# Seven block products for half of the output projection of an encoder block, with the last two gate groups regrouped

## Chip, cores and metric

The kernel runs on one core of a Trainium2 chip. The metric is device time of one execution in microseconds (us). A core has five engines that each run their own instructions in order and wait for one another by semaphores: PE (TensorE, matrix products), DVE (VectorE), ACT (ScalarE), POOL (GpSimd) and SP (SyncE, which here issues the transfers). PE writes into PSUM, eight banks of 512 f32 columns; the other engines must empty a bank before PE can write it again.

## The reference

One layer of an encoder block on 1024 tokens with 1024 channels, in f32:

```python
u = rms_norm(x, norm1_g)
proj = u @ w_in
q, k, v, cb, cc, ch, ga, gb = jnp.split(proj, split_pts, axis=-1)
...
y_a = neighbourhood_attention(q, k, v, rpb) @ w_attn_branch
y_b = short_gated_conv(cb, cc, ch, conv_w) @ w_conv_branch
merged = jax.nn.sigmoid(ga) * y_a + jax.nn.sigmoid(gb) * y_b
x = x + merged @ w_o
h = rms_norm(x, norm2_g) @ w_mlp_in
x = x + jnp.square(jax.nn.relu(h)) @ w_mlp_out
```

The change touches `merged` (gates and branches) and the product `merged @ w_o`, called the projection here: 1024 x 1024 by 1024 x 1024.

## The kernel before, in words

**Precision.** Every f32 operand is scaled by a power of two and split in two f16 parts, high and low. A product of two operands is three passes (high by high, high by low, low by high; `PASSES`, L479) that are added up in PSUM. The high part is an ACT copy with a scale, the low part a DVE `scalar_tensor_tensor` (scaled operand minus high part). A scale needs the largest element, or the sum of squares, of the whole operand over all 128 partitions: each engine makes a column of partial results, DVE casts it into a column of the tile `ones`, PE multiplies it by a matrix of ones (`all_sum`, L226, the matmul is L227), and DVE reads the sum back from PSUM (L230) and makes the power of two in four or five steps on single columns (`pow2`, L153, `pow2_half`, L467).

**Stages.** Input products, attention and short convolution; then eight gate groups n = 0..7 of 128 channels each; then the projection; then the two matrices of the MLP. Gate groups 1 to 7 and the MLP already use Strassen's scheme with seven products in place of eight (`seven`, L1273; one product is 12 matmuls of 512 or 256 columns); the projection doesn't.

**Gates.** For each n (L1342): seven products of 12 matmuls give both gates of the group for both halves of the tokens (`gate_units`, L1297). Their combination is on DVE (L1310 to L1313, L1319, L1326, L1327), the sigmoid on ACT (L1321). Then four branch groups of 12 matmuls (`branch_units`, L1331) give y_a and y_b of the group; DVE multiplies them by the gates (L1357) and adds the two (L1359) to `m`, the group's part of `merged`. `m_done` (L1290) takes the largest element of `m` and splits `m` into M[0] and M[1], the stationary operand of the projection, with a scale for each group. For n = 7 the four branch groups come first (L1368), the largest element is bounded from them (`bound`, L1373), and gate 7 comes last, so that its products can be multiplied in and split half by half (`last`, L1386).

**Weights.** Weights come as f32 pieces of 128 x 1024 into five rotating buffers `raw`; SP issues a load when an earlier piece has been split (`load_upto`, L261). w_o has two column halves of four pieces, cO[0] and cO[1]; each piece is reduced to its row maxima by DVE (`largest`, L357) and then split (L343, L330).

**Projection.** `proj(b, half)` (L1605): for a block b of 128 tokens and a half of 512 columns, 24 matmuls of 512 columns (8 channel groups, three passes), then DVE adds the result to x in X1 (L1610). The first half runs over b = 4, 5, 0, 1, 2, 6 (L1628 to L1635); channel group 7 of the first two blocks is put behind the other 42 matmuls. The ten other half-blocks (`tail`, L1637) run between the steps of the second norm, of `form_sums` (L1480), of the splits and transposes of the normalized rows, and of the first pieces of w_1 (`forms_m`, L1551; `prep1`, L1518).

**Order of the work.** Nothing is reordered after the program is written: each engine runs its instructions in the order in which the Python program emits them. Preparations are generators in two lists, `fg` and `bg`. `unit` (L233) emits one group of matmuls, then what was put off after the group before it (`late`: usually what empties its PSUM bank), and then moves `fg` by `steps` and `bg` by `ticks` steps. `apart` (L208) lets a generator wait for a count of groups before it emits its matmul with ones. `drain` and `flush` empty the lists. SP runs its transfers in the order of issue too, and one that waits holds those behind it.

Of the kernel before, what the change touches and what calls it, by code (L numbers as in the profile page):

```python
# [28 lines left out]
def plan():  # L29
# [9 lines left out]
    for n in range(8):  # L39
        p.append((("S" if n else "G", n), block("w_in", [(3072 + 128 * n, 128), (4096 + 128 * n, 128)], 4)))  # L40
        if n % 2 == 0:
            p += branch(n // 2)
# [57 lines left out]
def encoder_block(ctx: ExitStack, tc: tile.TileContext, x, weights, cols, gqk, rel, masks, out):  # L100
# [1183 lines left out]

    def m_split(n, m, s):
# [4 lines left out]
    def m_done(n, m):  # L1290
        mx, s = tmp(), tmp()
        V.tensor_reduce(sc[:, mx], m, axis=AX, op=OP.max, apply_absolute_value=True)
        yield
        yield from pow2(mx, 14, s, at(rowsM, n))
        yield from m_split(n, m, s)

    def gate_units(n, tail=None):  # L1297

        sg = w3p.tile([128, 4, 512], F32, name="sg")
# [18 lines left out]
        def post3(ps):  # L1318
# [9 lines left out]
            7: post7, 3: post3}, 2, 4 if n < 7 else 6, (1, 6, 2, 4, 5, 7, 3))  # L1328
        return sg

    def branch_units(n, post, mid=None):  # L1331
        j, cc = n // 2, (n % 2) * 128
        for g, act, ch in ((0, actA, cA[j]), (1, actB, cB[j])):
            built(ch)
            for half in range(2):
                ps = anybank()
                unit(ch_mms(ps, act, half, ch, 4, 256, cc),
                     lambda ps=ps, g=g, half=half, ch=ch: post(g, half, ps, sc[:, ch.inv]), 2, 4)
                if mid and g == 0 and half == 0:
                    mid()  # L1340

    for n in range(8):  # L1342
        built(cG if n == 0 else cS[n])
        if n < 7:
            bg.append(prep_s(n + 1))
        m = w3p.tile([128, 2, 512], F32, name="m", bufs=1)
        mf = m.rearrange("p a t -> p (a t)")
        if n < 7:
            sg = gate_units(n)
            if n:  # L1350
                sg = [sg[:, i] for i in range(4)]
            if n in (1, 3, 5):
                push(cA[n // 2 + 1], cB[n // 2 + 1])

            def post(g, half, ps, iv, sg=sg, m=m):
                t = sg[2 * half + g]
                V.scalar_tensor_tensor(t, ps, iv, t, op0=OP.mult, op1=OP.mult)  # L1357
                if g == 1:
                    V.tensor_tensor(m[:, half], sg[2 * half], t, op=OP.add)  # L1359
            branch_units(n, post, (lambda: turn_s(0, 2)) if n == 0 else None)  # L1360
            if n == 0:
                late.append(lambda: held.__setitem__(0, 0))
            late.append(lambda n=n, mf=mf: fg.append(m_done(n, mf)))
        else:
            push(cO[0])
            tick(4)
            y = w3p.tile([128, 4, 512], F32, name="gsum", bufs=1)
            branch_units(n, lambda g, half, ps, iv: A.activation(y[:, 2 * half + g], ps, AF.Copy, scale=iv))  # L1368
            settle()
            drain()  # L1370
            s7 = tmp()

            def bound():  # L1373
                mm, m2, mx = tmp(4), tmp(2), tmp()
                V.tensor_reduce(sc[:, mm], y, axis=AX, op=OP.max, apply_absolute_value=True)
                yield
                V.tensor_tensor(sc[:, m2], sc[:, mm.start:mm.start + 4:2], sc[:, mm.start + 1:mm.start + 4:2],
                                op=OP.add)
                V.tensor_reduce(sc[:, mx], sc[:, m2], axis=AX, op=OP.max)
                yield from pow2(mx, 14, s7, at(rowsM, 7))  # L1380
                for ch in cO:
                    ch.ready = True

            fg.append(bound())

            def last(sg, half):  # L1386
                o = slice(2 * half, 2 * half + 2)
                V.tensor_tensor(sg[:, o], sg[:, o], y[:, o], op=OP.mult)
                V.tensor_tensor(m[:, half], sg[:, 2 * half], sg[:, 2 * half + 1], op=OP.add)
                t = slice(512 * half, 512 * half + 512)  # L1390
                A.activation(M[0][:, 7, t], m[:, half], AF.Copy, scale=sc[:, s7])
                V.scalar_tensor_tensor(M[1][:, 7, t], m[:, half], sc[:, s7], M[0][:, 7, t],
                                       op0=OP.mult, op1=OP.subtract)

            gate_units(7, last)
            u2T = base.tile([128, 4, 2, 4, 512], F16, name="u2T", tag="U")
            c1[0].raw = [u2T[:, 3, i].rearrange("p k t -> p (k t)").bitcast(F32) for i in range(2)]
            for i in range(2):
                load_into(c1[0].raw[i], c1[0], i)
            r21 = u2T[:, 2, 0].rearrange("p k t -> p (k t)").bitcast(F32)  # L1400
            X1 = base.tile([128, 8, D], F32, name="x1", tag="Q")
            for b in range(8):
                SP.dma_start(X1[:, b], x[b * 128:(b + 1) * 128, :])
            load_into(r21, c1[1], 1)
            settle()
    drain()
    flush()
    side[0] = False

# [70 lines left out]
    def form_sums():  # L1480
        for _ in sums(fv[0], V):
            pass
# [543 lines left out]
```

## Time and profile before

| | |
|---|---|
| time, median of 3 runs | 1200.93 us (1200.65 to 1201.29) |
| the profiled execution's own time | 1201.78 us |
| its span, first to last instruction | 1200.0 us |
| granted PE clock | 1.00 throughout |

The profile is of one execution. Instructions carry the kernel's line (L1310), the engine, the operation, the tiles as out<-in, and the shape. In a timeline the columns are start and length in us; "x12" is the number of instructions merged in a row, and a bracket gives the engine's idle time before it with what ended it. In groups of instructions the last columns are busy us, mean ns of one, and idle time before. A matmul's end is modelled and reaches into the next one, so the distance between starts is the measure. Before, gate 7's first matmul starts at 514.33 and the projection's first at 532.48.

### The profile page before, as it was taken

What the parts mean: (1) busy time and instruction counts of PE and PEld (TensorE: products, weight loads), DVE (VectorE), ACT (ScalarE), POOL (GpSimd) and SP (SyncE); (2) the same over time, 40 slices, a digit from 0 to 9 for tenths busy, and PEclk for the clock granted to TensorE, in tenths of its full rate; (3) what the DMA queues carried; (4) which work ended last, traced back from release to release, by engine and by line L of the source; (5) the groups of instructions that cost most, each with busy time, mean ns of one, the idle gap of its engine ahead of it and who ended that gap; (6) DMA issues with size and microseconds to landing.
All of it is one profiled execution on the core that took longest, in us unless ns stands there. A gap on an engine that the chain in (4) does not pass through costs nothing.

```text
span 1200.0 us, 16982 instructions
## 1 busy us (share of the span) xinstructions
PE 1190.2 (99%) x6272; PEld 574.7 (48%) x6272; DVE 940.3 (78%) x1750; ACT 752.1 (63%) x1181; POOL 450.9 (38%) x296
## 2 busy tenths in 40 slices
PE   8999999999999999999999999999999999999998
PEld 7444444444444444444467444444444444444444
DVE  7987878899558786877888645645548999999998
ACT  7765668778654545337778778678675843746440
POOL 5610022322311203001014665565567561564562
DMA  7745547576641121234397445435466925435202
GB/s 259 201 153 126 107 96 145 124 163 117 135 121 58 54 70 36 71 116 165 60 170 195 174 142 192 160 130 193 153 242 220 356 73 193 158 120 214 105 36 105
DMA packets 162707, 171.25 MB, mean 143 GB/s; under 512 B 123328, under 2 KB 123840, under 8 KB 158528
## 3 DMA queue, kind: packets, MB, share of 16 engines
q1 hardware_dynamic: 162624, 170.17, 48.4%
q8 instruction: 49, 0.80, 0.3%
q14 instruction: 34, 0.28, 0.1%
HBM read 102.51 MB, written 37.75 MB: 117 GB/s over the span
## 4 chain that ended last, share of the span: by engine, by line
PE 84%; DVE 11%; ACT 2%; issue 1%; DMA 1%; SPq 0%; ACTq 0%
PE ps_d L236 27%; PE ps_s L236 24%; PE ps_o L236 20%; PE ps_d L1067 5%; PE ps_d L669 2%; PE ps_d L718 2%; PE ps_s L718 2%; DVE P L95 2%; PE ps_s L669 2%; DVE w_s L1234 1%; DVE sz L95 1%; DVE sc L95 1%; DVE w_ws L95 1%; DVE sg L1357 1%; DMA xt<-in_x 1%
## 5 line engine op out<-in xcount | busy, mean ns | idle before, releaser
L236 PEld LDWEIGHTS <-ops 128*128 128x128 f16 x1356 | 132.5, 98 | 157.3
L236 PEld LDWEIGHTS <-w 128*128 128x128 f16 x1368 | 132.8, 98 | 139.4
L1067 PE MATMUL ps_d<-uT,w_ws 128*128 128x512 f16 x576 | 128.0, 379 | 0.3 <-DVE cv L95 0.3
L236 PE MATMUL ps_s<-ops 128*128 128x512 f16 (+1 forms) x504 | 114.3, 376 | 0.0
L236 PE MATMUL ps_d<-ops 128*128 128x512 f16 x492 | 112.9, 379 | 0.0
L236 PE MATMUL ps_d<-u2T,w 128*128 128x512 f16 (+1 forms) x504 | 110.1, 371 | 0.0
L1847 ACT ACTIVATE ops<-hf,sc 128x2048 f16<-128x2048 f32 x26 | 52.0, 1998 | 84.8 <-PE ps_d L236 47.2
L1221 POOL TENSOR_TENSOR tsum<-raw 128x512 f32<-128x512 f32 x28 | 48.2, 1737 | 139.3 <-DVE v L1475 74.2
L1425 POOL TENSOR_TENSOR as<-as 128x512 f32<-128x512 f32 x60 | 82.9, 1382 | 41.6 <-ACT as L1707 38.1
L236 PEld LDWEIGHTS <-w_s 128*128 128x128 f16 x588 | 56.8, 98 | 69.0 <-DVE w_s L1234 1.2
L1067 PEld LDWEIGHTS <-w_ws 128*128 128x128 f16 x576 | 54.6, 98 | 65.6 <-issue 1.5
L236 PE MATMUL ps_o<-ops 128*128 128x512 f16 (+1 forms) x360 | 81.3, 375 | 0.0
L236 PE MATMUL ps_s<-u2x,w 128*128 128x512 f16 (+1 forms) x348 | 78.6, 375 | 0.0
L1849 DVE SCALAR_TENSOR_TENSOR ops<-hf,sc,ops 128x2048 f16<-128x2048 f32 x26 | 74.8, 2876 | 3.2 <-ACT ops L1847 2.2
L1099 ACT ACTIVATE raw<-raw,sc 128x256 f32<-128x256 f32 x164 | 67.5, 494 | 1.9 <-DMA raw<-in_weights 1.9
L1221 POOL TENSOR_TENSOR gsum<-raw 128x512 f32<-128x512 f32 x14 | 19.3, 1394 | 127.8 <-issue 53.6
L1238 ACT ACTIVATE w<-raw,sc 128x512 f16<-128x512 f32 (+1 forms) x28 | 24.6, 927 | 50.8 <-DVE sc L475 50.8
L1740 DVE TENSOR_TENSOR as<-ps_s,as 128x512 f32<-128x512 f32 x13 | 9.0, 692 | 57.9 <-ACT as L1759 57.9
L1321 ACT ACTIVATE sg<-sg,sc 128x2048 f32<-128x2048 f32 (+1 forms) x7 | 13.2, 1880 | 52.2 <-DVE sg L1319 52.2
L1863 POOL TENSOR_TENSOR raw<-raw 128x1024 f32<-128x1024 f32 x8 | 30.8, 3870 | 36.5 <-DVE ops L1857 36.5
L236 PE MATMUL ps_o<-u2T,w 128*128 128x512 f16 (+1 forms) x204 | 44.2, 366 | 0.0
L236 PEld LDWEIGHTS <-mH 128*128 128x128 f16 x304 | 29.6, 98 | 30.4
(393 smaller groups left out, 2664.2 us busy)
## 6 DMA issues: line engine op xcount, KB each, us to landing
raw<-in_weights SPq DMA_DIRECT2D x89, 512.0 KB, 5.2
hs<-as SPq DMA_DIRECT2D x16, 1792.0 KB, 8.7
hf<-hs SPq DMA_DIRECT2D x26, 1024.0 KB, 6.6
w2x<-in_weights SPq DMA_DIRECT2D x16, 512.0 KB, 7.6
raw<-in_weights SPq DMA_DIRECT2D x16, 384.0 KB, 3.7
xt<-in_x SPq DMA_DIRECT2D x8, 512.0 KB, 10.2
gs<-s SPq DMA_DIRECT2D x4, 1024.0 KB, 4.4
x<-in_x SPq DMA_DIRECT2D x8, 512.0 KB, 10.6
```

What stands on the lines that cost most here:

```text
L95: return f(out, *a, **kw)
L236: T.matmul(ps, l, r, start=a, stop=b)
L669: T.matmul(ps, UT[:, sa, k, b * 128:(b + 1) * 128], w, start=(kind, k) == ("hh", 0), stop=(kind, k) == ("hl", 7))
L718: T.matmul(vbank["q", b], UT[:, sa, k, b * 128:(b + 1) * 128], cQ.parts[:, sw, 512 * k:512 * k + 512], start=(k, n) == (0, 0), stop=(k, n) ...
L1067: T.matmul(ps, l, r, start=a, stop=b)
L1099: A.activation(v, v, AF.Copy, scale=sc[:, at(g, 4 * i + k)])
L1221: G.tensor_tensor(t[:, o], a, b, op=OP.add)
L1238: A.activation(o(0), w, AF.Copy, scale=sc[:, s])
L1425: sub.tensor_tensor(z[o], z[a], z[b], op=op)
L1847: A.activation(P[:, 1, 0], hf, AF.Copy, scale=sc[:, Rs])
L1849: V.scalar_tensor_tensor(P[:, 1, 1], hf, sc[:, Rs], P[:, 1, 0], op0=OP.mult, op1=OP.subtract)
L1863: G.tensor_tensor(w11[i2], w11[i2], w12[i2], op=OP.add)
```

## The change

1. **Branches of groups 6 and 7 first.** The loop over gate groups ends at n = 5. Then come all eight branch groups of n = 6 and 7 (`last_branches`), whose results are kept in four tiles `Y`, then gate 6 and gate 7 with no branches between them. Both are multiplied in half by half by `last`. The weights cA[3] and cB[3] are loaded ahead of gate 6's weights. `bound` now covers both groups.
2. **One scale for a pair of groups**, and Strassen's sums of `merged`: after each pair (2i, 2i+1) POOL forms four sums of 384 tokens in place (`m_sums`: they serve three of the four row blocks of each token half), ACT and DVE split them (`m_parts`), and SP stores them to memory in `MS`. Pairs 0, 1 and 2 are loaded again later; the sums of the last pair are made in `last_forms`, after gate 7, straight into their place. The gate tile `sg` has one buffer where it had two, and `m` holds a pair.
3. **w_o.** Scales come from sums of squares (ACT, `o_scale`), with the groups' scales applied afterwards, where they came from row maxima (DVE). The first half is split plain (`o_plain`, into the tile that held the convolution result) and, after four sums per piece on POOL, once more as sums (`W`). The second half (`prep_o1`) is prepared during the projection.
4. **Projection, first column half.** For the row pairs (0, 4), (1, 5), (2, 6): seven products in the order 1, 4, 2, 6, 7, 5, 3, each in two units of two row pairs and one, 12 matmuls of 256 columns for a row pair. `o_post` combines them into X1 on DVE, POOL and ACT. Row blocks 3 and 7 and the second column half stay as they were.
5. **Smaller moves.** The loads of w_1's first pieces (c1) go behind the third stored sum; w_1's first split waits for the end of the Strassen half (`o_half`) and takes another buffer; `form_sums` for three of four row pairs and the sums in `forms_m` go from DVE to POOL.

The core of the diff:

```diff
+    FORMS = ((3, 1, 3, OP.subtract), (1, 0, 1, OP.subtract), (0, 3, 0, OP.subtract), (2, 2, 0, OP.add))
...
+    def m_sums(m):
+        q = m.rearrange("p a h t -> p (a h) t")[:, :, 0:384]
+        for o, a, b, op in FORMS:
+            G.tensor_tensor(q[:, o], q[:, a], q[:, b], op=op)
+            yield
+        return q
+    def m_parts(q, t, s):
+        for a in (0, 2):
+            A.activation(t[:, a:a + 2, 0], q[:, a:a + 2], AF.Copy, scale=sc[:, s])
+            yield
+        for a in (0, 2):
+            V.scalar_tensor_tensor(t[:, a:a + 2, 1], q[:, a:a + 2], sc[:, s], t[:, a:a + 2, 0],
+                                   op0=OP.mult, op1=OP.subtract)
+            yield
...
+    def o_scale(ch, top, junk):
+        rm, rs, a, b, s = (cols_of("prep", i) for i in (4, 4, 1, 1, 1))
+        ch.inv = keep()
+        for p in range(4):
+            while len(ch.raw) <= p:
+                yield WAIT
+            A.activation(junk, ch.raw[p], AF.Square, accum_out=sc[:, at(rm, p)])
+            yield
+        while not o_ready[0]:
+            yield WAIT
+        ri = sc[:, rowsM.start:rowsM.start + 8:2]
+        for _ in range(2):
+            V.tensor_tensor(sc[:, rm], sc[:, rm], ri, op=OP.mult)
+        V.tensor_reduce(sc[:, a], sc[:, rm], axis=AX, op=OP.add)
+        c, mark = ones_col(), units[0]
+        V.tensor_copy(c, sc[:, a])
+        yield from apart(mark, 1)
+        yield from all_sum(c, b, anybank(), 1e-36)
+        yield from pow2_half(b, top, s, ch.inv)
+        V.tensor_scalar(sc[:, rs], ri, sc[:, s], None, op0=OP.mult)
+        yield
+        return rs
...
+    def prep_o():
...
+        for n in range(4):
+            yield from o_plain(ch, n, rs)
+            r = ch.raw[n].rearrange("p (f c) -> p f c", f=4)
+            for o, x_, y_ in ((0, 0, 1), (1, 1, 3), (3, 0, 3), (2, 3, 2)):
+                G.tensor_tensor(r[:, o], r[:, x_], r[:, y_], op=OP.add)
+            yield
+        while not gated[0]:
+            yield WAIT
+        W = wsp.tile([128, 4, 2, 1024], F16, name="w16_t", tag="ws")
+        WT.append(W)
+        for p in range(4):
+            r = ch.raw[p].rearrange("p (f c) -> p f c", f=4)
+            hi, lo = (W[:, :, w, 256 * p:256 * p + 256] for w in range(2))
+            A.activation(hi, r, AF.Copy, scale=sc[:, at(rs, p)])
+            yield
+            V.scalar_tensor_tensor(lo, r, sc[:, at(rs, p)], hi, op0=OP.mult, op1=OP.subtract)
+            done[0] += 1
+            load_upto(done[0] + 5)
+            yield
...
+    def last(n, m, sg, half):
+        V.tensor_tensor(sg[:, 2 * half], sg[:, 2 * half], Y[n, 0][:, half], op=OP.mult)
+        (G if n == 6 else V).tensor_tensor(sg[:, 2 * half + 1], sg[:, 2 * half + 1], Y[n, 1][:, half], op=OP.mult)
+        V.tensor_tensor(m[:, half], sg[:, 2 * half], sg[:, 2 * half + 1], op=OP.add)
+        if n == 7:
+            t = slice(512 * half, 512 * half + 512)
+            A.activation(M[0][:, 7, t], m[:, half], AF.Copy, scale=sc[:, s7])
+            V.scalar_tensor_tensor(M[1][:, 7, t], m[:, half], sc[:, s7], M[0][:, 7, t],
+                                   op0=OP.mult, op1=OP.subtract)
...
+    last_branches()
+    bg.append(prep_o())
+    settle()
+    fg.append(bound())
+    mp = w3p.tile([128, 2, 2, 512], F32, name="m", bufs=1)
+    built(cS[6])
+    gate_units(6, lambda sg, half: last(6, mp[:, 0], sg, half))
+    gated[0] = 1
+    built(cS[7])
+    late.append(lambda: fg.append(m_split(6, mp[:, 0].rearrange("p h t -> p (h t)"), s7)))
+    gate_units(7, lambda sg, half: last(7, mp[:, 1], sg, half))
...
+    for i in range(2):
+        SP.dma_start(SM[i], MS[:, i])
+    X1 = base.tile([128, 8, D], F32, name="x1", tag="Q")
+    for b in range(8):
+        SP.dma_start(X1[:, b], x[b * 128:(b + 1) * 128, :])
+    settle()
+    def last_forms():
+        q = yield from m_sums(mp)
+        yield from m_parts(q, SM[3], s7)
+        forming[0] += 1
+    fg.append(last_forms())
     drain()
...
+    SP.dma_start(SM[2], MS[:, 2])
+    for i in range(2):
+        load_into(c1[0].raw[i], c1[0], i)
+    load_into(r21, c1[1], 1)
...
-    push(cO[1])
+    bg.append(prep_o1())
...
+    PRODUCT = {1: (0, 0), 2: (1, 2), 4: (3, 6), 6: (4, 7), 7: (5, 5), 5: (7, 4), 3: (6, 3)}
...
+    for o in (1, 4, 2, 6, 7, 5, 3):
+        if o == 6:
+            while forming[0] < 4:
+                step()
+        for j, n in ((0, 2), (2, 1)):
+            ps = anybank()
+            mms = []
+            for c in range(n):
+                mms += o_mms(ps[:, 256 * c:256 * c + 256], o, j + c)
+            unit(mms, lambda ps=ps, o=o, j=j, n=n: o_post(o, ps, j, n, [acc[:, u, j:j + n] for u in range(3)]),
+                 5, 3 * n)
```

`PRODUCT` gives for each product its row sum and its weight sum. Row sums 0 to 3 are the plain parts of `merged` (even and odd channel group, first and second token half), 4 to 7 the sums of `m_sums`; weights 0 to 3 are plain quarters of a piece, 4 to 7 the sums in `W`. So product 1 needs no part of group 7, product 4 needs its second token half, product 2 its first.

More of the change, by code (lines that the diff above doesn't have):

```diff
@@ L1297, in gate_units, with prep_o1 @@
+    def prep_o1():
+        ch = cO[1]
+        P = ch.parts = wsp.tile([128, 2, 4096], F16, name="w16_ws", tag="ws")
+        rs = yield from o_scale(ch, 14, P[:, 1, :1024].bitcast(BF16))
+        for n in range(4):
+            yield from o_plain(ch, n, rs)
+            done[0] += 1
+            load_upto(done[0] + 5)
+            yield
+        ch.split = True
     def gate_units(n, tail=None):
-        sg = w3p.tile([128, 4, 512], F32, name="sg")
+        sg = w3p.tile([128, 4, 512], F32, name="sg", bufs=1)
@@ L1337, in branch_units @@
                 unit(ch_mms(ps, act, half, ch, 4, 256, cc),
-                     lambda ps=ps, g=g, half=half, ch=ch: post(g, half, ps, sc[:, ch.inv]), 2, 4)
+                     lambda ps=ps, g=g, half=half, ch=ch: post(g, half, ps, sc[:, ch.inv]), 2, 5 if n in (2, 4) else 4)
                 if mid and g == 0 and half == 0:
                     mid()
-    for n in range(8):
-        built(cG if n == 0 else cS[n])
-        if n < 7:
-            bg.append(prep_s(n + 1))
-        m = w3p.tile([128, 2, 512], F32, name="m", bufs=1)
-        mf = m.rearrange("p a t -> p (a t)")
[L1348 to L1405, printed above, removed]
@@ L1406, in encoder_block @@
+    for b in range(8):
[4 more added lines that the diff above has]
+        yield from m_parts(q, SM[3], s7)
+        forming[0] += 1
+    fg.append(last_forms())
     drain()
+    forced[0] = True
+    while not cO[0].split:
+        tick()
+    forced[0] = False
     flush()
@@ L1478, in low, with form_sums @@
         pair_done[0] = n + part
-    def form_sums():
-        for _ in sums(fv[0], V):
+    def form_sums(e=None):
+        for _ in sums(fv[0], e or G):
             pass
```

163 lines of the change are left out of this document (143 added, 20 removed).

## Prediction

> **What bounds the kernel now.** I read the page first, then the granted clock and busy time by stage, then the order of time around the projection, then the groups by shape for prices.
>
> ```profile
> span 1200.0 us, 16982 instructions
> PE 1190.2 (99%) x6272; PEld 574.7 (48%) x6272; DVE 940.3 (78%) x1750; ACT 752.1 (63%) x1181; POOL 450.9 (38%) x296
> PE 84%; DVE 11%; ACT 2%; issue 1%; DMA 1%; SPq 0%; ACTq 0%
> ```
>
> TensorE (PE) is busy for 99% and holds 84% of the chain that ended last. So a change pays only through fewer or shorter matmuls, and costs only where PE has to wait. The stages concerned, gate group 7, the first six half-blocks of the projection and its ten later blocks, are these (columns: stretch, PE, PE loads, DVE, ACT, POOL, granted clock, DMA):
>
> ```profile
> 514.30:532.40 18.10, 18.10 (x86) 8.24 (x85) 13.38 (x32) 7.80 (x12) 0.00 (x0) 1.00 0.16 47
> 532.40:563.50 31.10, 31.10 (x148) 14.13 (x146) 21.89 (x38) 19.57 (x36) 5.08 (x4) 1.00 0.64 242
> 563.50:615.40 51.90, 51.90 (x243) 23.51 (x241) 44.11 (x81) 35.39 (x49) 0.00 (x0) 1.00 0.46 87
> ```
>
> PE never waits there, at full clock. Below, zero is the projection's first matmul (532.48).
>
> **The gain: fewer matmul columns.** The spacing of matmuls comes from starts, since their ends are modelled:
>
> ```profile
> 529.89 2.75 PE L236 MATMUL ps_s<-s4T,w_s 128*128 128x512 f16 x12
> 532.48 0.59 PE L236 MATMUL ps_o<-w_ws,mH 128*128 128x512 f16 x2
> 537.01 0.59 PE L236 MATMUL ps_d<-w_ws,mH 128*128 128x512 f16 x2
> ...
> 615.44 1.47 PE L236 MATMUL ps_o<-u2T,w 128*128 128x256 f16 x12
> 616.75 1.47 PE L236 MATMUL ps_d<-u2x,w 128*128 128x256 f16 x12
> ```
>
> From 532.48 to 537.01 lie 21 matmuls of 512 columns: 0.2157 us each. From 615.44 to 616.75 lie 12 of 256: 0.1092 each. Removed are six half-blocks of 24, 144 x 0.2157 = 31.1 us. Added are seven products, three row pairs, 12 matmuls of 256: 252 x 0.1092 = 27.5 us. Gain: **3.6 us**. One page speaks against it: the Trainium skill, "TensorE: Matmul & The Clock Gate", section "Back-to-back issue gap", states that in a real stream of loads and matmuls the spacing is about 81 ns at 128 columns and 131 ns at 512. By it the products take at least 252 x 0.081 = 20.4 against 144 x 0.131 = 18.9 us, a loss of 1.5 us (an estimate from that page); the rows above, 215.7 and 109.2 ns, do not bear those figures out.
>
> **The cost: the end of the gates.** In the old order four branch groups (48 matmuls, 10.4 us) lay between gates 6 and 7; now gate 7 follows gate 6 at once, and w_o is split twice (four plain pieces, then four pieces of sums). All engines run in the order in which the kernel emits, so I laid that order out by hand. Prices:
>
> ```profile
> 531.88 0.69 DVE L1310 TENSOR_TENSOR sg<-ps_d,sg 128x512 f32<-128x512 f32 x1
> 533.92 0.69 DVE L1313 TENSOR_TENSOR sg<-ps_o,sg 128x512 f32<-128x512 f32 x1
> 538.57 0.75 DVE L1392 SCALAR_TENSOR_TENSOR mL<-m,sc,mH 128x512 f16<-128x512 f32 x1 [0.79 <-ACT mH L1391]
> 539.24 0.68 DVE L1319 TENSOR_TENSOR sg<-ps_s,sg 128x512 f32<-128x512 f32 x1
> 543.88 0.75 DVE L1392 SCALAR_TENSOR_TENSOR mL<-m,sc,mH 128x512 f16<-128x512 f32 x1 [0.79 <-ACT mH L1391]
> ...
> 534.65 1.15 ACT L1315 ACTIVATE sg<-sg,sc 128x1024 f32<-128x1024 f32 x1 [3.82 <-DVE sg L1313]
> 537.81 0.72 ACT L1391 ACTIVATE mH<-m,sc 128x512 f16<-128x512 f32 x1 [2.02 <-DVE m L1389]
> ```
>
> ```profile
> L880 POOL TENSOR_TENSOR cv<-cv,z 128x256 f32<-128x256 f32 x16 | 12.6, 820 | 0.3
> L904 POOL TENSOR_TENSOR bT<-cv,bT 128x256 f16<-128x256 f32 x16 | 11.0, 719 | 9.4 <-ACT bT L95 9.4
> L517 POOL TENSOR_TENSOR biasm<-bias,mk 128x384 f32<-128x384 f32 x8 | 8.9, 1115 | 62.8 <-DVE sc L460 40.0 <-DVE sc L95 16.5 <-DVE bias L95 5.1
> L1425 POOL TENSOR_TENSOR as<-as 128x512 f32<-128x512 f32 x60 | 82.9, 1382 | 41.6 <-ACT as L1707 38.1
> L1221 POOL TENSOR_TENSOR u2x<-u2T 128x512 f32<-128x512 f32 x2 | 2.5, 1273 | 65.3 <-ACT u2T L1099 65.3
> L1221 POOL TENSOR_TENSOR tsum<-raw 128x512 f32<-128x512 f32 x28 | 48.2, 1737 | 139.3 <-DVE v L1475 74.2 <-ACT raw L1099 65.1
> ```
>
> ```profile
> L1238 ACT ACTIVATE w_s<-raw,sc 128x1024 f16<-128x1024 f32 x6 | 6.8, 1133 | 0.0
> L1108 ACT ACTIVATE gsum<-raw 128x1024 f32<-128x1024 f32 x12 | 12.6, 1053 | 0.2
> L1108 ACT ACTIVATION_READ_ACCUMULATOR gsum<-raw 128x1 f32 x12 | 2.2, 187 | 0.0
> L1234 DVE SCALAR_TENSOR_TENSOR w_s<-raw,sc,w_s 128x1024 f16<-128x1024 f32 x6 | 7.7, 1284 | 1.7 <-ACT w_s L1238 1.7
> ```
>
> A gate is seven groups of 12 matmuls, 18.1 us, so gate 6's sixth product ends at -20.7, and DVE goes on in this order. Gate 6, half 1: four combinations 2.7 (531.88 to 534.61), wait for the sigmoid 1.2, product 0.7, wait for POOL's product 0.7 (taken as 1.33, between its 1.27 and 1.38), sum 0.7, three small steps of w_o's scale 0.5: -14. First w_o piece: wait for ACT's high part 1.2, low part 1.3: -11.5. Half 0: 0.7, sigmoid 1.2, product 0.7, then 1.9 for POOL, whose product stands behind the piece's four sums (4 x 0.78, between 0.72 and 0.82), sum 0.7: -6.2. Group 6's split 1.2 + 1.3 and the second piece's low part 1.3: -2.4. POOL then has 12 sums left, 9.4 us, to +7.0; the last of the four sum pieces takes ACT 1.2 and DVE 1.3: **+9.6**. Only behind it in DVE's queue stands gate 7's combining, which ran at -0.6 before. DVE's own work from -20.7 to there is 19.7 us, so -1.0 is the earliest.
>
> From there the old rows give the rest. Half 1 took 531.88 to 539.32, 7.4 (0.2 more, its product is now two): +17.3. Half 0 took 539.24 to 544.63, 5.4 (0.2 more): +22.9. The fourth row sum on POOL, 1.1 (384 wide): +24. ACT's high part of it, 768 wide, between 0.72 and 1.15, taken as 0.93: +25. Behind that in ACT's queue stand the second w_o half's four squares, 4 x (1.05 + 0.19) = 5.0: +30. They were absent before, when DVE reductions did this.
>
> **Where PE meets it.** The scale of w_o's second half is summed over partitions by a one-column matmul with ones, in PE's own order:
>
> ```profile
> 524.69 0.17 PE L227 MATMUL ps_d<-ones 128*128 128x1 bf16 x1
> 524.92 0.16 DVE L230 TENSOR_SCALAR sc<-ps_d 128x1 f32<-128x1 f32 x1 [1.93 <-PE ps_d L227]
> 550.92 0.16 DVE L372 CAST ones<-sc 128x1 bf16<-128x1 f32 x1
> L227 PE MATMUL ps_s<-ones x1: 163/163/163, 553.2 to 553.2; 128*128 128x1 bf16 x1
> ```
>
> Before, for that half, DVE wrote the column at 550.92 (+18.4) and PE came to it at 553.2 (+20.7), four blocks into the projection. Now it is emitted one unit after the squares, and the first product's two units hold only 36 x 0.1092 = 3.9 us. The squares end at +30, five small DVE steps of 0.2 end at +31.0. PE waits **27.1 us** there. Inside the wait, and so free, lie the other new waits: product 4 needs group 7's half 1 (+17.3), product 2 its half 0 (+22.9). Queued behind the ones matmul is all further PE work; nothing on another engine needs PE meanwhile, so the wait is paid once.
>
> Bounds of the wait: with POOL's sums free it is 20.7; at 1.36 times their price (1737 over 1273 ns for one shape) 30.2. The Trainium skill, "GPSIMD Engine Reference", section "Key points", states that POOL shares its SBUF interfaces with VectorE and meets contention from DVE instructions with two SBUF inputs; the spread of that shape agrees, and by it the sum would go to the dearer end, 1227.6.
>
> **What I cost at nothing.** Transfers: SP now sends two stored row sums before x's eight blocks, the third and w_1's first loads after them.
>
> ```profile
> L259 SPq DMA_DIRECT2D u2T<-in_weights x3: 328/423/424, 532.4 to 542.6; - x3
> DMA to landing us min/median/max: 6.5/8.4/10.1
> DMA to landing us min/median/max: 9.3/10.6/11.4
> ```
>
> (the first landing row is w_1's, the second x's). SP is held by w_o's loads until +9.6. The third row sum goes where the gates' tiles lay, so I let it wait for their last user, +26; at 6.5 to 10 us it lands by +36, while PE, released at +31.0, comes to it at +39.6 (8.6 us later). If PE came without the wait, at +12.4, this transfer would cost it up to 24. Gates 0 to 5: per pair of groups POOL gets 7.1 us, ACT 1.9, DVE 0.6.
>
> ```profile
> 400.00:450.00 50.00, 49.88 (x236) 22.51 (x234) 36.95 (x78) 25.29 (x41) 5.07 (x5) 1.00 0.20 63
> ```
>
> A pair lasts 57 us and each engine has room, with eight PSUM banks ahead of PE; without that cover 0 to 2 us a pair. Moving the branches ahead issues the same groups; their weights are loaded one stage earlier. w_1's first split now comes after the Strassen half, into the later blocks, where three of four form sums go from DVE to POOL (4 x 1.38 against 4 x 0.69, 2.8 us later per row pair):
>
> ```profile
> L1425 DVE TENSOR_TENSOR form<-form 128x512 f32<-128x512 f32 x12 | 8.3, 690 | 0.3
> ```
>
> DVE, busy 44.1 of 51.9 there, gains 3 x 2.8 and the four other sums that leave it: 0 to +4, taken as 0, since the last pair stays on DVE.
>
> **Sum.** The profiled execution took 1201.78, its span 1200.0 and 1.8 around it. 1201.78 - 3.6 + 27.1 = 1225.3; the median of the runs is 0.85 under it: **1224.5**.
>
> **Rivals.** The last of them rests on the length of a weight load:
>
> ```profile
> L236 PEld LDWEIGHTS <-ops 128*128 128x128 f16 x1356 | 132.5, 98 | 157.3
> ```
>
> 1. *DVE isn't late* (0.20). If POOL's sums and ACT's steps fit into DVE's gaps, gate 7 is combined at -2.6 to +3, the ones matmul waits 15 to 20.7: 1212 to 1218. For it: DVE is busy 13.4 of 18.1 in the old gate 7. Against it: 19.7 us of work in 18.
> 2. *Faster: the closing of gate 7 is covered* (0.06). If the emission interleaves otherwise than I read it, so that group 7's halves, the row sums and the squares are done while PE still has other work, PE meets no wait: 1197.4. It decides at +7.5, the 3.9 of the first product plus the 3.6 gained: a column of ones written before that makes the change pay. Against it: even without any lateness, half 0, row sum, squares and small steps after gate 7's end take 5.6 + 1.1 + 0.9 + 5 + 1 = 13.6.
> 3. *More is late* (0.15). POOL's form sums delay the first MLP groups too, by 2.8 per row pair in a chain of three, or POOL is dear: 1228 to 1236.
> 4. *Narrow matmuls pay for their weights* (0.02). A load is 98 ns against 109 between starts; unhidden, 252 x 0.098 adds 24.7: 1249. The 615.44 rows, same width with loads, speak against it. It is what the Trainium skill, in the section cited above, gives as the cause of its 81 ns.
>
> **Numbers.** Forecast 0.57, 1218 to 1231 (20.7 of wait to 30.2 with 4 for the later blocks). The range 1209 to 1232 adds rival 1 whole, with 3 us for a shorter chain, and part of rival 3. This kernel's measurement tells about 0.2% (2.4 us) from no change. Faster 0.06, same 0.01 (a wait that happens to be near 3.6), slower 0.93.
>
> **What would show it.** Right: PE idle once for 20 to 30 us, some 4 us after the projection's first matmul, released by DVE's cast into ones; DVE's combining of gate 7 some 10 us after that gate's last matmul; 256-wide matmuls 0.109 apart. Wrong: PE waiting elsewhere (row sums landing, w_1's first parts), no idle PE at all, or squares ahead of gate 7's closing on ACT.

## The result

The changed kernel takes 1254.99 us (median of 4 runs, 1252.73 to 1255.82); the kernel before took 1200.87 beside it (4 runs, 1200.65 to 1201.29). The ratio is 1.0447, with a 95% interval of 1.0429 to 1.0465. The forecast was 1224.5, with a range from 1209 to 1232: the direction was right, but the loss of 54 us is more than twice the 24 forecast.

Line numbers below are those of the changed kernel, mostly two more than before as far as the gates: the ones matmul is L229, all other matmuls of these stages L238. Zero is again the projection's first matmul, now at 546.84. The page of the changed kernel first (span, busy time, the granted clock in 40 slices, the chain that ended last by engine):

```profile
span 1253.5 us, 17322 instructions
PE 1197.1 (96%) x6380; PEld 589.1 (47%) x6380; DVE 947.4 (76%) x1734; ACT 774.3 (62%) x1208; POOL 531.7 (42%) x360
PEclk9999999999998999986899999999999999999999
PE 76%; DVE 13%; issue 4%; ACT 3%; POOL 2%; DMA 1%; SPq 0%; ACTq 0%; DVEq 0%; POOLq 0%
```

PE is idle for 56 us instead of 10, and the clock row has dips where before it had none in these stages. What PE waited for, from the view of waits (line that waited, releaser, total us, times, longest):

```profile
PE ps_s L229 <- DVE ones L1353: 32.3, 1, 32.3
PE ps_o L229 <- DVE ones L1082: 9.5, 2, 5.8
PE ps_s L229 <- DVE ones L1082: 3.7, 1, 3.7
PE ps_d L229 <- DVE ones L1353: 2.6, 1, 2.6
```

All five new waits stand at a ones matmul whose column DVE has not written yet: in gates 2 and 4 (3.7 each, the column of the pair's gate scale, L1082), in gate 6 (2.6, w_o's first half), after product 1 (32.3, w_o's second half, L1353) and after product 4 (5.8, w_1's first scale). By stage (stretch, PE, PE loads, DVE, ACT, POOL, granted clock, DMA share, GB/s), the last gate, the long wait with product 1, the other products, and the rest of the projection:

```profile
528.74:546.84 18.10, 18.10 (x85) 8.19 (x84) 10.25 (x14) 9.11 (x9) 8.07 (x8) 1.00 0.00 0
546.84:583.26 36.42, 4.10 (x38) 3.52 (x37) 20.03 (x26) 13.55 (x18) 16.29 (x15) 0.62 0.68 246
583.26:612.20 28.94, 23.18 (x174) 18.88 (x174) 15.76 (x36) 15.96 (x30) 14.98 (x12) 0.83 0.17 63
612.20:670.00 57.80, 57.80 (x297) 28.83 (x296) 39.64 (x55) 35.90 (x49) 23.91 (x17) 1.00 0.44 79
```

In the second stretch no engine is full: DVE is busy 20.0 of 36.4, POOL 16.3, ACT 13.6. It is a chain, handed from one to another. In the third the clock is 0.83. Behind 612 nothing is lost. DVE's part of the chain, from its timeline:

```profile
559.87 1.28 DVE L1387 SCALAR_TENSOR_TENSOR w_t<-raw,sc,w_t 128x1024 f16<-128x1024 f32 x1 [2.00 <-ACT w_t L1385]
561.07 0.69 DVE L1418 TENSOR_TENSOR sg<-ps_d,sg 128x512 f32<-128x512 f32 x1
...
567.82 0.75 DVE L1491 SCALAR_TENSOR_TENSOR mL<-m,sc,mH 128x512 f16<-128x512 f32 x1 [0.79 <-ACT mH L1490]
...
574.18 0.75 DVE L1491 SCALAR_TENSOR_TENSOR mL<-m,sc,mH 128x512 f16<-128x512 f32 x1 [0.79 <-ACT mH L1490]
...
582.45 0.36 DVE L1350 TENSOR_TENSOR sc<-sc 128x4 f32<-128x4 f32 x2 [3.56 <-ACT w_ws L1344]
582.85 0.16 DVE L1351 TENSOR_REDUCE sc<-sc 128x1 f32<-128x4 f32 x1
583.04 0.16 DVE L1353 CAST ones<-sc 128x1 bf16<-128x1 f32 x1
```

The last split of w_o's sums ends where gate 7's combining (L1418) begins, at +14.2; group 7's halves are there at +21.7 and +28.1; then come the last row sum, the squares on ACT (L1344) and the column, written at +36.4. Behind the wait the matmuls run at half speed for a while, which the starts show:

```profile
583.88 0.63 PE L238 MATMUL ps_o<-w_t,mH 128*128 128x256 f16 x2
584.30 0.42 PE L238 MATMUL ps_o<-w_t,mL 128*128 128x256 f16 x1
...
587.11 0.38 PE L238 MATMUL ps_o<-w_t,mH 128*128 128x256 f16 x2
587.33 0.27 PE L238 MATMUL ps_o<-w_t,mL 128*128 128x256 f16 x1
```

Two matmuls take 0.42 us at 583.88 and 0.22 at 587.11: 0.21 against 0.11 each. The account below counts every start from 335 us on against full-speed spacing, which makes a wait up to 0.2 us longer than the view of waits does: gates 2 and 4, 7.8 of wait and 4.6 of half speed (15 and 9 matmuls); gate 6, 2.8; w_o's second scale, 32.5 and 1.5; w_1's scale, 5.9 and 2.8. Together 57.9, less the 3.6 gained: 54.3. Between the medians 54.1 was measured, and 53.5 between the two profiled executions.

### The profile page after: what moved, and what is told of

Read it like the earlier page. It is cut to its first block, busy times and chain, and to the rows that moved or that the text cites. A ratio compares the mean times of both kernels' runs of the same rounds, so it can differ in the third digit from the quotient of the medians.

```text
span 1253.5 us, 17322 instructions
## 1 busy us (share of the span) xinstructions
PE 1197.1 (96%) x6380; PEld 589.1 (47%) x6380; DVE 947.4 (76%) x1734; ACT 774.3 (62%) x1208; POOL 531.7 (42%) x360
## 4 chain that ended last, share of the span: by engine, by line
PE 76%; DVE 13%; issue 4%; ACT 3%; POOL 2%; DMA 1%; SPq 0%; ACTq 0%; DVEq 0%; POOLq 0%
PE ps_d L238 25%; PE ps_s L238 21%; PE ps_o L238 17%; PE ps_d L1069 5%; PE ps_d L671 2%; PE ps_d L720 2%; PE ps_s L720 2%; DVE P L97 1%; PE ps_s L671 1%; POOL raw L1376 1%; DVE sz L97 1%; DVE w_s L1236 1%; DVE sc L97 1%; DVE w_ws L97 1%; DMA xt<-in_x 1%
## 5 line engine op out<-in xcount | busy, mean ns | idle before, releaser
L238 PEld LDWEIGHTS <-ops 128*128 128x128 f16 x1356 | 132.3, 98 | 157.4
L238 PEld LDWEIGHTS <-w 128*128 128x128 f16 x1368 | 132.7, 98 | 139.6
L238 PE MATMUL ps_s<-ops 128*128 128x512 f16 (+1 forms) x504 | 114.4, 377 | 0.0
L238 PE MATMUL ps_d<-ops 128*128 128x512 f16 x492 | 112.9, 379 | 0.0
L238 PE MATMUL ps_d<-u2T,w 128*128 128x512 f16 (+1 forms) x504 | 110.2, 372 | 0.0
L238 PEld LDWEIGHTS <-w_s 128*128 128x128 f16 x588 | 56.9, 98 | 71.2 <-issue 2.9
L238 PE MATMUL ps_o<-ops 128*128 128x512 f16 (+1 forms) x360 | 81.3, 376 | 0.0
L238 PE MATMUL ps_s<-u2x,w 128*128 128x512 f16 (+1 forms) x348 | 78.6, 376 | 0.0
L238 PEld LDWEIGHTS <-mH 128*128 128x128 f16 x280 | 27.8, 100 | 53.3 <-issue 32.5
L1945 DVE TENSOR_TENSOR as<-ps_s,as 128x512 f32<-128x512 f32 x13 | 9.0, 692 | 57.9 <-ACT as L1964 57.9
L1515 POOL TENSOR_TENSOR m<-sg 128x512 f32<-128x512 f32 x5 | 7.3, 1451 | 106.6 <-DVE sg L1513 88.6
L238 PE MATMUL ps_o<-u2T,w 128*128 128x512 f16 (+1 forms) x204 | 44.2, 367 | 0.0
```

What stands on the lines that cost most here:

```text
L238: T.matmul(ps, l, r, start=a, stop=b)
```

## The experiments

Each kernel below ran once, with a profile, beside a run of the kernel before on the same chip (1200.86, 1201.02 and 1201.44 in the three batches). The changed kernel's own four times lie 3.1 us apart, so a difference of 3 us between single times shows nothing by itself; what the waits in the profiles show is surer. The theory at the start was that **place** is the cause: ones matmuls stand in PE's order before their columns can be ready. The rival was that the **work** added for the products is, and the ones matmul is only the first to meet it.

### Single edits of place

```diff
-            s, ch.inv = yield from scale_of(ch.sum, 9, 2)
+            s, ch.inv = yield from scale_of(ch.sum, 9, 3)
```

> Only the gates' pair scale changes: its ones matmul is emitted three units after the branch sums instead of two, one unit of 12 matmuls (12 x 0.2157 = 2.6 us of PE work) later. Theory (PE stands at a ones matmul whose column isn't written yet): the two waits of 3.88 us at 378 and 442 us fall to 1.3 each, and the half-speed matmuls behind them (15 and 9 of them, 2.95 and 1.68 us) go, since after the wait of 2.81 us at 520.5 there were none: 2 x 2.6 + 4.6 = 9.8 us, 1245. Rival (what is late is the split behind the scale, not the place of the matmul): the wait moves to the next product of the gate and the time stays within 2 us of 1255.

Measured 1249.54. Both waits and their half-speed matmuls are gone, and others stand there: in each of the two gates 0.5 and 1.4 us at products that wait for splits of w_s, later 0.7 at another ones matmul, and gate 6's own wait, now followed by 1.3 of half speed. 5.5 of the 9.8 us came back. Neither side was wholly right.

```diff
-        yield from apart(mark, 1)
+        yield from apart(mark, 1 if ch is cO[0] else 8)
```

> Only the ones matmul of w_o's second half moves: eight units after its squares instead of one. Theory A (nothing but the place of this matmul holds PE): the wait of 32.5 us goes nearly whole and the time falls by 25 to 34, to 1221 to 1230. Theory B (gate 7's closing is late for the products as well): PE goes on to product 4, which needs group 7's half 1, written at +21.7 after the projection's first matmul, then to product 2, which needs half 0 (+28.1), then to the third row sum's way through memory (landing some +37): the wait is split into several and only 10 to 16 us come back, 1239 to 1245.

Measured 1252.37. The waits of PE in that kernel, the two longest entries:

```profile
PE ps_o L229 <- DVE ones L1082: 23.7, 3, 19.4
PE ps_s L238 <- ACT mH L1490: 9.9, 1, 9.9
```

The 32 us at w_o's scale are gone, and PE spends them elsewhere: 16.4 in product 4 (for the splits of w_o's sums, and 9.9 for ACT's high part of group 7's half 1), with 1.4 of half speed, and 19.4 at the next ones matmul, w_1's, ahead of product 2. Only 2.6 us came back, less than single times can tell apart. The place of this one matmul as the whole cause of the long wait fell here.

```diff
-    gated[0] = 1
     built(cS[7])
...
-    gate_units(7, lambda sg, half: last(7, mp[:, 1], sg, half))
+    gate_units(7, lambda sg, half: (last(7, mp[:, 1], sg, half), gated.__setitem__(0, half)))
```

> The split of w_o's sums is held until gate 7's first half has been combined, instead of until gate 6 is done, so it stands behind gate 7's combining in DVE's and ACT's queues. If the order in the queues is what makes gate 7 late: its combining comes at 0 to +1 instead of +14.2, the halves some 8 to 12 us earlier, w_o's ones matmul waits 20 to 27 instead of 32.5, 1243 to 1250. If the sums come in between the halves on POOL and hold them there instead, the halves gain less than 4 and the time stays at 1251 to 1257, or product 4 waits for its weights in place of its row sums.

Measured 1255.83. Against the projection's first matmul (here at 546.50) group 7's halves were there at +11.2 and +20.6, 10.5 and 7.4 us earlier, and the column came no earlier (+37.1):

```profile
581.67 1.06 ACT L1344 ACTIVATE w_ws<-raw 128x1024 bf16<-128x1024 f32 x1 [6.13 <-DMA raw<-in_weights]
582.63 0.19 ACT L1344 ACTIVATION_READ_ACCUMULATOR w_ws<-raw 128x1 f32 x1
```

The fourth piece of w_o's second half can be loaded only when the last split of the first half's sums has freed its buffer. With that split moved back, ACT's last square waits for the transfer. The time is inside the range given for no gain, for another cause than the one named there.

### Several edits of place

```diff
+        yield from apart(mark, 1 if ch is cO[0] else 8)
...
+        s, ch.inv = yield from scale_of(ch.sum, 9, 1 if q else 6)
...
+        s, ch.inv = yield from scale_of(ch.sum, 9, 6)
```

> As the kernel with w_o's ones matmul eight units after its squares, and w_1's two first scales too: their ones matmuls wait for six units' worth of 256-wide work (6 x 24 matmuls) instead of one. Theory (PE went from one ones matmul to the next; behind both stand the products' own data): the wait of 19.8 us at w_1's ones goes, the short waits before products 4 and 2 (17.8 us in all) stay, and PE then stands at product 6 until the third row sum has come back from memory, sent at 578.6 in that kernel and landing some 5 us later, 7 us before that ones matmul ran: 1245. Rival (w_1's scale is needed by then anyway): PE stands later at w_1's first quads for the same time, 1252.

Measured 1250.67, nearer to the rival's time, though not by its mechanism. The 17.8 given to products 4 and 2 were product 4's alone, half speed included; product 2 adds 1.3. What PE waited for besides:

```profile
PE ps_s L238 <- DVE x L1803: 5.9, 1, 5.9
PE ps_d L238 <- DMA u2x<-ms: 5.0, 1, 5.0
```

The second row is the third row sum's transfer, as expected. The first is new: a PSUM bank that DVE has not emptied, because DVE stands at w_1's column, waiting for ACT, with the products' results queued behind.

```diff
-            s, ch.inv = yield from scale_of(ch.sum, 9, 2)
+            s, ch.inv = yield from scale_of(ch.sum, 9, 3)
...
-    for i, o in ((0, 0), (1, 1), (3, 2)):
+    for i, o in ((0, 0), (1, 1), (3, 2), (2, 3)):
...
-    for i in range(2):
+    for i in range(3):
         SP.dma_start(SM[i], MS[:, i])
+    for i in range(2):
+        load_into(c1[0].raw[i], c1[0], i)
```

These lines, with the late ones matmuls and the moved split from above, are the five edits; `r21`, the buffer of a piece of w_1, takes the place that the third row sum had.

> Five edits together, all of order and place, none of work: the pair scale's ones one unit later; w_o's sums split behind gate 7's first half; w_o's and w_1's ones matmuls late; the third row sum kept beside the other two, so that its transfer needn't wait for the gates' tiles; w_1's first loads ahead of x. If the loss is order (each wait is for something that stands behind other work), PE waits at gate 7's half 0 and at the last split of w_o's sums only, some 19 us after the first product, and 8 us in the gates: 1222 to 1230. If it is the amount of work on DVE, ACT and POOL between gate 6 and the products, no more than 10 us come back against the kernel as changed: 1245 or above.

Measured 1247.72: 7 us back of 54, within the 10 that the rival allows. In this kernel DVE's longest wait is one at the four-element steps of w_o's scale (the first row; the others are PE's waits). PE waits longest, 15.8, for the splits of w_o's sums, which the moved split puts behind gate 7, and then for PSUM banks that ACT and DVE have not emptied:

```profile
DVE sc L1350 <- ACT w_ws L1344: 14.5, 1, 14.5
```

```profile
PE ps_s L238 <- ACT w_t L1385: 15.8, 2, 8.7
PE ps_o L238 <- ACT as L1806: 5.4, 1, 5.4
PE ps_s L238 <- DVE x L1800: 4.9, 1, 4.9
```

```diff
-    for o in (1, 4, 2, 6, 7, 5, 3):
+    for b in (3, 7):
+        proj(b, 0, None, two)
+    unit(two[0][0][:21], None, 5, 6)
+    unit(two[1][0][:21], None, 5, 6)
+    for o in (1, 2, 4, 6, 7, 5, 3):
```

> As the five edits together, and before the first product PE gets the first 21 of 24 matmuls of the two plain half-blocks (3 and 7), which need neither sums nor the last gate group; products 2 and 4 change places. 42 x 0.2157 = 9.1 us of cover. If PE waits only for gate 7's closing, all of it comes back: 9 us under the five edits, some 1213 to 1221. If something on another engine is late on its own path (the splits of w_o's sums, w_1's scale), less than 4 us come back.

Measured 1249.77. In this kernel block 6 is normalised before its second half has been added, so its output is not the reference's. The cover worked where it stood (PE ran 10 us longer before its first wait in the projection), but w_o's ones matmul then waited 13.5 and a PSUM bank 10.8: nothing was gained.

```diff
+        s, ch.inv = yield from scale_of(ch.sum, 9, 3)
...
+        yield from apart(mark, 1 if ch is cO[0] else 8)
...
+    for i in range(3):
         SP.dma_start(SM[i], MS[:, i])
```

> The whole work of the changed kernel, with four of the five edits of place (the pair scale one unit later, both late ones matmuls, the third row sum and w_1's first loads early), and w_o's sums split before gate 7's closing again, so that the last raw piece of w_o's second half is not late. Gates: 5 to 6 us back, as in the run with that edit alone. Products 4 and 2 wait 18 us as before, the wait for the third row sum (5.1) goes; what DVE does behind the squares decides the rest: 1234 to 1240. If 1246 or above, the order that the change has is about as good as any of these, and the amount of work is the cause.

W_1's late ones matmuls and early loads, as above, belong to it too. Measured 1244.49, the best of the kernels that have the products whole, 10.5 under the changed kernel, between the two bounds given. The longest waits left are for group 7's half and for PSUM:

```profile
PE ps_s L238 <- ACT mH L1490: 9.9, 1, 9.9
PE ps_o L238 <- ACT as L1807: 4.4, 1, 4.4
PE ps_s L238 <- DVE x L1801: 3.8, 1, 3.8
```

### Work left out

```diff
-        q = yield from m_sums(m)
-        t = w3p.tile([128, 4, 2, 384], F16, name="mform", bufs=1)
-        yield from m_parts(q, t, s)
         forming[0] += 1
...
-    for o in (1, 4, 2, 6, 7, 5, 3):
+    unit(two[0][0][:21])
+    unit(two[1][0][:21])
+    for mm, fin in two:
+        unit(mm[21:], fin, 6, 4)
+    for b in (0, 1, 2, 6):
+        proj(b, 0)
```

> The change without its first part: branches ahead of both gates and scales from squares stay, but there are no row sums, no sums of w_o's quarters and no products; the six half-blocks are computed plainly, 144 matmuls of 512, in the old order with 42 of them as cover. The waits in gates 2, 4 and 6 stay (15 us with the half-speed matmuls). If the sums are what makes gate 7 late: DVE combines it at -1 to +1, half 0 is there at +13, squares on ACT end at +18, and the ones matmul, now at +10 to +15, waits 5 to 9 us: 1220 to 1227, so that the products cost some 30 us for their 3.6. If the squares and the early branches cost the most, 1235 or above.

Measured 1205.54, far under every range given: the clock row of its page shows nines throughout. PE's waits at ones matmuls, and two rows of DVE's timeline (zero is 533.56 there):

```profile
PE ps_o L229 <- DVE ones L1349: 2.4, 1, 2.4
PE ps_s L229 <- DVE ones L1082: 0.5, 1, 0.5
PE ps_o L229 <- DVE ones L1082: 0.5, 1, 0.5
```

```profile
534.13 0.68 DVE L1400 TENSOR_TENSOR sg<-ps_d,sg 128x512 f32<-128x512 f32 x1
...
551.43 0.16 DVE L1349 CAST ones<-sc 128x1 bf16<-128x1 f32 x1
```

Gate 7's combining begins at +0.6 and the column is written at +17.9, as expected; PE comes to it only at +15.5, because 72 wide matmuls lie ahead of it and not 36 narrow ones. I had carried the waits of gates 2, 4 and 6 over, as if the branches or the squares caused them; they belong to the products' row sums. So all that this kernel keeps of the change (the early branches, the pair's scale, the scales from squares, the smaller moves) costs 4.5 us, and the products with what they need 49.5.

```diff
-            for o, x_, y_ in ((0, 0, 1), (1, 1, 3), (3, 0, 3), (2, 3, 2)):
-                G.tensor_tensor(r[:, o], r[:, x_], r[:, y_], op=OP.add)
```

> Leaves out the four POOL sums of each w_o piece, so that the split pieces hold the plain quarters and the output is no longer the reference's; all else is as in the changed kernel. Theory (DVE reaches gate 7's combining late because it waits for the splits of sums, which wait for POOL): the combining moves from +14.2 to +1 to +3 after the projection's first matmul, the wait at w_o's ones matmul falls from 32.5 to 20 to 22, and the time to 1242 to 1245. Rival (DVE's own work sets it: 12 splits of 1.3 and gate 6's closing): the wait falls by no more than 5, 1250 or above.

Measured 1245.27. The combining came at +5.2 and the ones matmul waited 23.5: the theory's direction, 2 us short of it. What is left ahead of the combining are DVE's own splits, as the next kernel shows.

```diff
-            r = ch.raw[n].rearrange("p (f c) -> p f c", f=4)
...
-            V.scalar_tensor_tensor(lo, r, sc[:, at(rs, p)], hi, op0=OP.mult, op1=OP.subtract)
...
-            return WT[0][:, w - 4, s, 256 * i:256 * i + 256]
+            return cO[0].parts[:, s, 1024 * i + 256 * (w - 4):1024 * i + 256 * (w - 4) + 256]
```

> Leaves out the sums of w_o's quarters and their split altogether (12 POOL sums, 4 splits on ACT and on DVE); products 4, 6, 7 and 5 read the plain quarters, so the output isn't the reference's. DVE should combine gate 7 at +0.6 as without the products, instead of +14.2; the ones matmul's column comes 13 to 14 us earlier, and it waits 18 to 20 us instead of 32.5: 1240 to 1243. If the combining is held by something else (gate 6's closing, w_o's plain pieces), 1246 or above.

Measured 1241.19, the combining at +0.6, as expected:

```profile
PE ps_s L229 <- DVE ones L1353: 18.7, 1, 18.7
```

The same kernel with both late ones matmuls and the early transfers:

```diff
+        yield from apart(mark, 1 if ch is cO[0] else 8)
...
+        s, ch.inv = yield from scale_of(ch.sum, 9, 1 if q else 6)
...
+    for i in range(3):
         SP.dma_start(SM[i], MS[:, i])
```

> As the kernel without w_o's sums and their split, and with both late ones matmuls and the third row sum and w_1's loads sent early. What is left then is gate 7's closing alone: half 1 at +8, half 0 at +13.4, the last row sum's parts at about +18. PE should wait some 4 us at product 4, 1 to 2 at product 2 and 1 at product 6 and, if DVE then stands at a column's small steps with the products' results behind it, some 5 for PSUM: with the gates' 15 us, 1215 to 1224. If it stays above 1230, another resource holds the products than those named so far.

Measured 1234.62, above the range. Products 4 and 2 waited 5.5 as expected. Two PSUM waits (4.4 and 4.1) came where one was allowed for, half-speed matmuls took 5.0 behind them and 4.4 in the gates, and 3.2 were lost in the first MLP groups, which expect PE later.

```diff
-        for o, a, b, op in FORMS:
-            G.tensor_tensor(q[:, o], q[:, a], q[:, b], op=op)
-            yield
...
-            for o, x_, y_ in ((0, 0, 1), (1, 1, 3), (3, 0, 3), (2, 3, 2)):
-                G.tensor_tensor(r[:, o], r[:, x_], r[:, y_], op=OP.add)
```

> Leaves out all of POOL's new sums: the row sums of the four group pairs and the sums of w_o's quarters (what is split and multiplied is then the plain data, so the output isn't the reference's). All splits, transfers, products and scales stay. Theory (POOL's sums make the columns late, in the gates as at their end): without the w_o sums alone the time was 1245.3; without the row sums too the two waits of 3.88 us in gates 2 and 4 fall to the 0.7 that they are without the products, the half-speed matmuls behind them go (4.6 us), and the last row sum's 1.8 us leave the chain to the squares: about 13 us less, 1230 to 1234. Rival (the splits on ACT and DVE hold DVE's queue in the gates): those waits stay above 2.5 and the time above 1240.

Measured 1234.03: POOL's new sums are worth 21 us. In gates 2 and 4 the wait fell to 2.1, not to 0.7; the rest is the row sums' split on DVE, two steps of 1.0 us ahead of the column. And POOL's sums do not only make others wait for them. The same four-piece split of a branch weight, grouped (minimum, median and maximum ns of one), first in the changed kernel and then without POOL's sums:

```profile
L332 DVE SCALAR_TENSOR_TENSOR w_wa<-raw,sc,w_wa x8: 471/988/1220, 374.8 to 441.6; 128x256 f16<-128x256 f32 x8
```

```profile
L332 DVE SCALAR_TENSOR_TENSOR w_wa<-raw,sc,w_wa x8: 480/484/488, 374.1 to 434.5; 128x256 f16<-128x256 f32 x8
```

While POOL adds, this DVE instruction takes twice its time. One place of the changed kernel shows it too: in gate 2 the first three of the four lie beside POOL's row sums and take 0.76, 1.22 and 1.22 us; the fourth begins after POOL's last and takes 0.47. The other branch weight's eight splits, w_wb's, come when POOL adds nothing and take 480 ns in both kernels. The Trainium skill, "GPSIMD Engine Reference", section "Key points", says that POOL shares its SBUF interfaces with VectorE and meets contention from DVE instructions with two SBUF inputs, as this one has; the pair of rows agrees, and shows that DVE loses as well.

## Why the prediction was right in direction and wrong in size

**The gain: right.** The products' matmuls start 0.109 apart at full clock (the 587.11 rows) and PE runs 3.6 us less.

**The cost, gate 7's closing: right in mechanism, one term too small.** The term that was too small, and the first step that failed, is "POOL then has 12 sums left, 9.4 us":

```profile
L1376 POOL TENSOR_TENSOR raw<-raw x12: 722/726/1702, 544.9 to 557.9; 128x256 f32<-128x256 f32 x12
```

The median of 0.73 us is below the 0.78 taken, but the longest takes 1.70, and the twelve together 13.7 us, 1.15 each. Seven of them take 0.72 to 0.73. The other five take 1.58 to 1.70, and each of these five runs beside a DVE split of w_o, as this pair does:

```profile
551.97 1.35 DVE L1387 SCALAR_TENSOR_TENSOR w_t<-raw,sc,w_t 128x1024 f16<-128x1024 f32 x1 [2.00 <-ACT w_t L1385]
552.32 1.58 POOL L1376 TENSOR_TENSOR raw<-raw 128x256 f32<-128x256 f32 x1
```

Five times 0.88 is 4.4, and the whole term was 4.3 too small. The prediction had dearer sums only as a bound, spread evenly over all twelve; here the price falls on those that begin while DVE is splitting. So the combining came at +14.2 and not at +9.6. From there the forecast holds: half 1 was there 7.5 after it (forecast 7.7), half 0 13.9 (13.3), and the column 8.3 behind half 0 (8.1). The wait became 32.5 instead of 27.1: 5.4 of the error, 4.6 of it from the combining. The dearer bound, 1.36 times the price, comes near: 0.78 x 1.36 is 1.06. (How that bound becomes a wait of 30.2 is not worked out; 27.1 + 0.36 x 9.4 is 30.5.) The other bound, 20.7 with POOL's sums free, was met: in the kernel without POOL's sums PE waited 20.4 there.

**"Inside the wait, and so free": right as far as it went.** With the ones matmul moved, product 4 alone waits 16.4. It also means that the long wait couldn't be repaired by moving one matmul; the prediction did not claim it.

**"What I cost at nothing": the other step that failed.** Three things in it were not free. PE waiting elsewhere was one of the prediction's signs of being wrong, and of the places named there w_1's first parts are the third below.

- Gates 0 to 5, "with eight PSUM banks ahead of PE": 0 to 2 us a pair were bounded, 3.9 and 3.9 came in gates 2 and 4, with 4.6 of half speed. I weighed busy time per pair against a pair's 57 us. What counted was the one place in PE's order where the pair's gate scale is summed: the row sums' split on DVE stands ahead of its column, and POOL's sums stretch DVE's steps before it. PSUM banks cover nothing there, since the ones matmul itself waits. The run without products (0.7) and the run without POOL's sums (2.1) show both halves of this.
- W_o's first scale, in gate 6: 2.8, the same kind of place, which the prediction does not name. The runs without products and without all of POOL's sums do not have it; the runs that leave out w_o's sums alone still do (2.8), so it comes from the row sums on POOL.
- W_1's scale behind product 4: 5.9 and 2.8 of half speed. The prediction followed the third row sum through SP's queue, and not what stands behind it there: w_1's first two pieces. ACT, whose row of the changed kernel follows, begins on them after the long wait has ended; their squares and DVE's splits of w_o's second half stand before the column.

```profile
584.71 3.30 ACT L1101 ACTIVATE u2T<-u2T,sc 128x256 f32<-128x256 f32 x8 [2.29 <-DMA u2T<-in_weights]
```

The later blocks, taken as 0, cost 0.

**Not counted at all: the clock.** 8.9 us of the loss are matmuls at half speed behind four of the five waits. Forecast and account meet when these are put in: 1224.5 + 5.4 + 12.4 + 2.8 + 1.5 + 8.7 = 1255.3.

**The rivals.** The first (DVE not late, 15 to 20.7 of wait) is what the kernel without w_o's sums and their split shows: 18.9. The second's point, a column before +7.5, was far off even there (+22.8). The third named more lateness and was the nearest: its second condition, that POOL is dear, held; its first, lateness in the later blocks, did not. The fourth is ruled out by the spacing of 0.109.

**What stays open.** No kernel that has the products whole came under 1244.5. How far a wholly rearranged end of the gates could go was not tried; with w_o's sums at no cost and the edits of place it was still 1234.6.

## What to carry to other kernels

A scheme that saves matmuls pays only if its sums and splits fit beside work that PE still has; here 3.6 us of PE stood against a chain of 36 us through DVE, ACT and POOL at the one place with the least cover. For every matmul that only sums a scale, ask where it stands in PE's order and when the last instruction ahead of its column on DVE ends: busy shares say nothing about that. And before moving such a matmul, list what PE would meet next: here the next two places took 16.4 and 19.8 us, together more than the 32.5 removed.

## What was not expected of the hardware

After a wait PE can run at half speed for 7 to 28 matmuls, and the wait's length alone does not decide it. In the kernel without POOL's sums two waits of nearly the same length stand 59 us apart (the ones matmul and the group behind it):

```profile
380.56 0.16 PE L229 MATMUL ps_o<-ones 128*128 128x1 bf16 x1 [1.93 <-DVE ones L1082]
380.59 2.75 PE L238 MATMUL ps_d<-qD,w_wa 128*128 128x512 f16 x12
```

```profile
439.75 0.16 PE L229 MATMUL ps_s<-ones 128*128 128x1 bf16 x1 [1.95 <-DVE ones L1082]
439.78 4.08 PE L238 MATMUL ps_d<-qD,w_wa 128*128 128x512 f16 x12
```

Behind the first, twelve matmuls take 2.75 us; behind the second, 4.08. The wait of 2.8 us in gate 6 was followed by none in the changed kernel and by nine with one matmul moved elsewhere. Waits of 3.9 us and more were followed by it in gates 2 and 4 of every run that had them. The Trainium skill, "TensorE: Matmul & The Clock Gate", section "Part 1: The HAM clock gate", gives a free-running window of about 3.4 us after which an idle array falls to half its clock. A free-running window would let two equal waits end differently, as these rows do, though no row here shows the window itself; that 2 us of idle can be enough does not follow from the length stated there.

The second was what DVE's splits and POOL's sums do to each other: the splits of the branch weights took 988 against 484 ns, and POOL's sums of w_o 1.58 to 1.70 against 0.73 us, both shown above.
